# Sample attention of a hybrid decoder step taken by pairs of tokens, with the whole-array steps of a run ahead of its column products

## The chip, the cores and the metric

The kernel runs on one core of a Trainium2 chip. The metric is the device time of one execution in microseconds (us): the median of three timed runs of the kernel before is 2583.79 us (2583.14 to 2585.33). Engines are named as in the profile: PE is TensorE's matmul (PEld its weight load), DVE VectorE, ACT ScalarE, POOL GpSimd, SP SyncE.

## The reference

One step of a two-layer decoder trunk is computed for a prompt of 256 tokens and for 8 sample sequences of 4 new tokens each, which share all weights. Layer 0 mixes tokens by sparse attention: an indexer picks 256 keys for each query token out of 2048 cached ones (in pages) and the sequence's new ones, and grouped attention (16 heads on 4 key heads) runs over the picked rows alone. Layer 1 mixes by a convolution module; each layer is followed by a feed-forward block. The part that the change touches is the attention itself, of the samples and of the prompt:

```python
def attend_selected(q, k_sel, v_sel, valid):
    qg = q.reshape(tq, N_KV_HEADS, N_HEADS // N_KV_HEADS, HEAD_DIM)
    s = jnp.einsum('tngd,tsnd->tngs', qg, k_sel) * (HEAD_DIM ** -0.5)
    s = jnp.where(valid[:, None, None, :], s, -jnp.inf)
    p = jax.nn.softmax(s, axis=-1)
    o = jnp.einsum('tngs,tsnd->tngd', p, v_sel)
    return o.reshape(tq, N_HEADS * HEAD_DIM)

def one_seq(q_s, qi_s, wi_s, ki_s, k_new, v_new, pages):      # each sample sequence
    idx, valid = index_select(qi_s, wi_s, ki_s, pos_new, key_pos, k_sel)
    ...
    k_s = jnp.where(in_past, cache_k[phys, off], k_new[new_idx])
    v_s = jnp.where(in_past, cache_v[phys, off], v_new[new_idx])
    return attend_selected(q_s, k_s, v_s, valid)
```

Everything is float32. The outputs are the trunk's result, the new keys, values and indexer keys, and the new convolution states.

## The kernel before, in words

Activations are held with features on partitions and all 288 tokens (256 of the prompt, 32 of the samples) in the free dimension. Weights are streamed from HBM in slabs of 512 KB. `K.pump` loads slabs ahead (up to `k.R` of them) and splits each into a high and a low part (up to `k.S` ahead): ACT writes `wh` (L179), DVE, or POOL for a few slabs, writes `wl` (L181). A product with a weight is three PE products (L258 to L260). Each engine runs its instructions in the order in which the program emits them.

The projections of layer 0 and the selection of keys come first. Then comes the attention stage, with PSUM divided into eight banks: three named `tr`, two `sc`, two `m` and one `q`. Its work is of two kinds.

- **The samples.** For each of 32 tokens (8 sequences `b`, 4 tokens each) POOL gathers 256 selected rows of keys and values from the cache (two gathers of 128 rows, L719) into one of 11 buffers. `keys(t)` transposes the gathered keys on PE: two blocks, `c` = 0 and 1, of four 128x128 transpositions (L1340), each block in a `tr` bank, copied to `KT` by ACT for block 0 (L1345) and by DVE for block 1 (L1343). `scores(t)` multiplies with the token's queries, each key head into 16 rows of a 32-row strip of one `sc` bank (L1361); the first token of a sequence also puts a mask there (L1353, from 32 rows of `selB` and `mbS`) and the scores of the new keys (L1356). Such products use 16 or 32 columns of the array: the program places them as column tiles of 128x32, four side by side, and the mask as a row tile. After the fourth token `values(b)` takes the softmax of the sequence: maximum on DVE (L1369, L1370), exponential with its sum on ACT (L1372), reciprocal on DVE (L1374), three transpositions of the result on PE (L1378, L1379) into an `m` bank, copied by ACT (L1389) and DVE (L1387) to `PTz` and by DVE to `zn` (L1390), then the product with the new values (L1395, tiles of 32x32) and with the gathered ones, token by token (L1402, column tiles). The sum is scaled on DVE to `os` (L1407), transposed (L1411) and copied to the output `ot` (L1414).
- **The prompt.** The generator `filler` has eight units, four key heads for each of two blocks of 128 queries. `qk` adds a mask and multiplies queries with keys (L1281, L1282) into a `tr` bank, DVE takes maxima (L1284, L1285), ACT the exponentials (L1287, 128 wide in the first four units, 256 wide in two parts in the others); `norm` scales them on DVE (L1263, L1265), `turn` transposes them on PE (L1294) for a copy by ACT (L1296), and `weigh` multiplies with the values (L1304) into the `q` bank, copied by ACT (L1307). All of these PE steps use the whole array.

The two kinds are woven by hand. A loop over tokens emits for each block of `keys` one step of the pending `values` generators and `fill(FILL)`, which adds `FILL` = 0.44 us to an account and emits pieces of `filler` (each of 0.6 to 1.5 us by the author's figures) as long as the account is positive; after the token's two blocks come the scores of the token before. At token 24 three slabs of the next product's weights are split in one go. After the last token the rest of `values` and `filler` is emitted; `split_o` (L1461, L1462) then splits the output for the product with `w_attn_out`, which starts as soon as its first row block is split.

Everything after that, about 85% of the time, is products with weights; these lines are the same before and after.

Of the kernel before, what the change touches and what calls it, by code (L numbers as in the profile page):

```python
# [40 lines left out]
FILL = 0.44  # L41
# [592 lines left out]
def trunk(ctx, tc, a, o, stages=9):  # L634
# [226 lines left out]
    def prepare():  # L861
# [305 lines left out]
    vs = ap.tile([32, 512], F32, name="vs")  # L1167
# [27 lines left out]
    def turn_v(gi):  # L1195

        for tt in range(3):
# [4 lines left out]
            dst = (vt[:, tt] if tt < 2 else vs)[:, 256 * gi:256 * gi + 256]  # L1202
# [49 lines left out]
    nc.sync.dma_start(o["v"][TP:], vs)  # L1252
# [78 lines left out]
    KT, SC = {}, {}  # L1331

    def keys(t):

        kt = cp.tile([128, NKV, KSEL_S], F32, name="KT", bufs=2)
        for c in range(2):
            p = bank("tr", 3)
            g = kvt[t][:, c]
            for h in range(NKV):
                nc.tensor.transpose(p[:, h * 128:(h + 1) * 128], g[:, h * 128:(h + 1) * 128], ident)  # L1340
            dst, src = kt[:, :, c * 128:(c + 1) * 128], p[:, :512].rearrange("p (h s) -> p h s", h=NKV)
            if c:
                nc.vector.tensor_copy(dst, src)  # L1343
            else:
                nc.scalar.activation(dst, src, AF.Copy)  # L1345
            yield
        KT[t] = kt

    def scores(t):
        b, i = t // TS, t % TS  # L1350
        if i == 0:
            SC[b] = p = bank("sc", 2)
            nc.tensor.matmul(p[:, :KSEL_S + 32], selB[96:128, b], mbS[96:128], start=True, stop=False,  # L1353
                             skip_group_check=True)
# [4 lines left out]
        p, kt = SC[b], KT.pop(t)  # L1359
# [4 lines left out]
    def values(b):  # L1364
# [6 lines left out]
        yield 1  # L1371
        nc.scalar.activation(P, p[:, :KSEL_S + 32], AF.Exp, bias=mx, scale=SCALE, accum_out=sm)  # L1372
        yield 1
        nc.vector.reciprocal(sm, sm)  # L1374
        yield 1
# [5 lines left out]
        zn = cp.tile([32, 128], F32, name="zn")  # L1381
        for c in range(2):
# [3 lines left out]
            if c:  # L1386
                nc.vector.tensor_copy(dst, src)  # L1387
            else:
                nc.scalar.activation(dst, src, AF.Copy)  # L1389
        nc.vector.tensor_copy(zn, p[:32, 256:384])  # L1390
        yield
        yield
        po = bank("m", 2)
        for h in range(NKV):
# [33 lines left out]
    def step():  # L1428
        for g_ in list(vq):
            if next(g_, 0) == 0:  # L1430
                vq.remove(g_)
# [602 lines left out]
```

## Time and profile before

| what | value |
|---|---|
| median of three timed runs | 2583.79 us (2583.14 to 2585.33) |
| the profiled execution's own time | 2567.41 us |
| its span, first to last instruction | 2565.6 us |
| busy PE, DVE, ACT, POOL in the span | 99%, 63%, 46%, 25% |
| granted TensorE clock, mean | 0.994 |
| attention stage, first key transposition to the first product of `w_attn_out` | 262.13 to 373.79 us |

The profile is of one execution; its time is 1.8 us above its span, and 16 us below the median of the timed runs. In a row of the timeline stand the start, the duration from there to the end of the last of the instructions taken together, the engine, the line, the operation, out<-in, the shape and the count; in brackets the idle time of the engine before and what ended it. PE's instructions overlap: from the start of one row to the start of the next is what the first takes of the engine, and its duration is longer. An fp32 product stands as two records, a transposition as one.

### The profile page before, as it was taken

The page shows a single profiled execution, that of the slowest core. Times are in us where ns is not written, and L with a number is a line of the kernel's source. Part 1 is how long each engine was busy: PE and PEld are TensorE (multiplying, and loading weights), DVE is VectorE, ACT ScalarE, POOL GpSimd, SP SyncE. Part 2 cuts the span into 40 slices and gives each one's busy share as a digit, 9 for nine tenths or more (in the row PEclk, how much of TensorE's full clock was granted, in tenths as well). Part 3 has the DMA queues.
Part 4 walks back from the last instruction along what each step waited for, and adds up shares of the span by engine and source line. Part 5 has one row for each costly group of instructions (what it writes and reads, how often), then busy time and mean ns, then how long its engine had stood idle before and what let it go on. Part 6 is the DMA issues. An engine that isn't in the chain of part 4 may idle for free.

```text
span 2565.6 us, 48371 instructions
## 1 busy us (share of the span) xinstructions
PE 2527.9 (99%) x19614; PEld 2437.1 (95%) x19614; DVE 1612.3 (63%) x2490; ACT 1171.6 (46%) x1858; POOL 654.1 (25%) x917
## 2 busy tenths in 40 slices
PE   9999999999999999999999999999999999999997
PEld 8889669999999999999999887999999999999997
DVE  5678556776665455555669997778555444555554
ACT  4464444554443334444446444656444333444444
POOL 2153732522221100101245564352111000111123
PEclk9999999999999999999999999999999999999999
DMA  9835955564545545556455655555555455555653
GB/s 347 209 127 189 344 206 204 160 204 160 169 161 173 164 159 171 161 169 172 163 164 177 176 162 182 164 163 164 170 163 168 165 157 172 164 165 164 171 165 103
DMA packets 151503, 454.80 MB, mean 177 GB/s; under 512 B 26112, under 2 KB 46512, under 8 KB 150000
## 3 DMA queue, kind: packets, MB, share of 16 engines
q1 hardware_dynamic: 138736, 400.04, 49.3%
q0 software_dynamic: 12016, 51.09, 5.8%
q8 instruction: 153, 2.51, 0.4%
q14 instruction: 70, 0.57, 0.1%
q10 hardware_dynamic: 528, 0.59, 0.1%
HBM read 438.37 MB, written 13.30 MB: 176 GB/s over the span
## 4 chain that ended last, share of the span: by engine, by line
PE 91%; DVE 5%; ACT 2%; POOL 1%; issue 1%; DMA 0%; SPq 0%; ACTq 0%; DVEq 0%; POOLq 0%
PE pt L260 26%; PE pt L259 26%; PE pt L258 26%; PE pg L258 2%; PE pg L260 2%; PE pg L259 2%; DVE wl L181 2%; PE tr L1340 1%; PE pt L1820 1%; PE m L1402 1%; DVE cy L1804 1%; PE pg L925 1%; PE sc L1361 1%; ACT wh L179 1%; PE q L1304 0%
## 5 line engine op out<-in xcount | busy, mean ns | idle before, releaser
L181 DVE TENSOR_TENSOR wl<-raw,wh 128x1024 fp32r<-128x1024 f32 (+1 forms) x707 | 882.7, 1251 | 752.1 <-ACT wh L179 748.6
L179 ACT ACTIVATE wh<-raw 128x1024 fp32r<-128x1024 f32 (+1 forms) x726 | 760.8, 1051 | 839.4 <-PE pt L259 691.5
L260 PE MATMUL pt<-xh,wl 128*128 128x288 f32 (+1 forms) x3520 | 1040.4, 296 | 3.4 <-DVE wl L181 3.3
L258 PE MATMUL pt<-xh,wh 128*128 128x288 f32 (+1 forms) x3520 | 1042.5, 296 | 0.9 <-ACT xh L1461 0.9
L259 PE MATMUL pt<-xl,wh 128*128 128x288 f32 (+1 forms) x3520 | 1042.5, 296 | 0.1
L258 PEld LDWEIGHTS pt<-xh,wh 128*128 128x128 f32 x3520 | 663.4, 188 | 7.8 <-issue 5.8
L260 PEld LDWEIGHTS pt<-xh,wl 128*128 128x128 f32 x3520 | 666.1, 189 | 5.0 <-DVE wl L181 5.0
L259 PEld LDWEIGHTS pt<-xl,wh 128*128 128x128 f32 x3520 | 664.0, 189 | 0.5 <-DVE xl L1462 0.3
L260 PE MATMUL pt<-hh,wl 128*128 128x288 f32 (+1 forms) x1664 | 495.2, 298 | 0.0
L259 PE MATMUL pt<-hl,wh 128*128 128x288 f32 (+1 forms) x1664 | 493.7, 297 | 0.0
L258 PE MATMUL pt<-hh,wh 128*128 128x288 f32 (+1 forms) x1664 | 492.8, 296 | 0.0
L1577 POOL COPY sto<-gpad 128x2 f32<-128x2 f32 x88 | 85.1, 967 | 970.2 <-ACT gpad L1570 970.1
L259 PEld LDWEIGHTS pt<-hl,wh 128*128 128x128 f32 x1664 | 313.9, 189 | 0.2
L258 PEld LDWEIGHTS pt<-hh,wh 128*128 128x128 f32 x1664 | 313.4, 188 | 0.2
L260 PEld LDWEIGHTS pt<-hh,wl 128*128 128x128 f32 x1664 | 312.8, 188 | 0.0
L258 PE MATMUL pg<-xh,wh 128*128 128x288 f32 (+1 forms) x528 | 164.9, 312 | 2.2 <-ACT xh L283 1.2
L260 PE MATMUL pg<-xh,wl 128*128 128x288 f32 (+1 forms) x528 | 157.6, 298 | 1.4 <-DVE wl L181 1.3
L259 PE MATMUL pg<-xl,wh 128*128 128x288 f32 (+1 forms) x528 | 157.5, 298 | 0.1
L1581 ACT ACTIVATE s<-y,pvec 128x304 f32<-128x304 f32 x88 | 48.5, 551 | 161.0 <-DVE y L1576 161.0
L258 PEld LDWEIGHTS pg<-xh,wh 128*128 128x128 f32 (+1 forms) x528 | 99.8, 189 | 11.9 <-issue 7.9
L259 PEld LDWEIGHTS pg<-xl,wh 128*128 128x128 f32 (+1 forms) x528 | 99.6, 189 | 3.6 <-issue 2.6
L260 PEld LDWEIGHTS pg<-xh,wl 128*128 128x128 f32 (+1 forms) x528 | 99.8, 189 | 3.1 <-DVE wl L181 3.1
(367 smaller groups left out, 2285.7 us busy)
## 6 DMA issues: line engine op xcount, KB each, us to landing
raw<-w SPq DMA_DIRECT2D x713, 512.0 KB, 3.5
xt<-spread SPq DMA_DIRECT2D x60, 136.0 KB, 4.0
kid<-kvt POOLq DMA_DIRECT2D x4, 1024.0 KB, 6.4
kvt<-kid SPq DMA_DIRECT2D x8, 512.0 KB, 11.4
x<-xT POOLq DMA_DIRECT2D x1, 2304.0 KB, 9.9
raw<-w SPq DMA_DIRECT2D x6, 384.0 KB, 3.0
out_y<-x SPq DMA_DIRECT2D x16, 144.0 KB, 1.8
hist<-scT POOLq DMA_DIRECT2D x4, 544.0 KB, 5.6
```

What stands on the lines that cost most here:

```text
L179: nc.scalar.activation(wh[:, :n], r[:, :n], AF.Copy)
L181: eng.tensor_tensor(wl[:, :n], r[:, :n], wh[:, :n].bitcast(F32), op=OP.subtract)
L258: nc.tensor.matmul(out, wh[:, c:c + w], xh, start=st, stop=False)
L259: nc.tensor.matmul(out, wh[:, c:c + w], xl, start=False, stop=False)
L260: nc.tensor.matmul(out, wl[:, c:c + w], xh, start=False, stop=sp)
L925: nc.tensor.matmul(p[:, :512], qb[:, pr], kx[pr][:, 512 * i:512 * i + 512], start=True, stop=True)
L1340: nc.tensor.transpose(p[:, h * 128:(h + 1) * 128], g[:, h * 128:(h + 1) * 128], ident)
L1361: nc.tensor.matmul(p[32 * h:32 * h + 16, :KSEL_S], qz[b % 2][:, i, h], kt[:, h], start=False, stop=(i == TS - 1), skip_group_check=True)
L1402: nc.tensor.matmul(po[32 * h:32 * h + 16, :128], z[:, c, i, h], g[:, 512 + h * 128:640 + h * 128], start=False, stop=(i == TS - 1 and c == ...
L1577: nc.gpsimd.tensor_copy(sto[:, j, 0:2], gp[:, 256:258])
L1581: nc.scalar.activation(s[:, :304], y[:, :304], AF.Silu, bias=k.par(bc, j))
L1804: nc.vector.scalar_tensor_tensor(acc, src, w, pl if q_ == NACT else acc, op0=OP.mult, op1=OP.add)
```

## The change

The loop over tokens becomes a loop over pairs of tokens (`p_`). A pair first emits all steps that use the whole array and then all column products:

- both tokens' blocks of `keys` (four times four transpositions); in a sequence's first pair, between them, the mask (now a product of all 128 rows, with zeros written into the upper 96 rows of `selB` and `mbS` by POOL), the exponential of the sequence before, its reciprocal and the three transpositions of the softmax, and the transposition of `os` for the sequence two before;
- then `fill` with 1.7 us of `filler` (0.8 us where no keys are left);
- then the products with values for two tokens of the sequence before, and the scores of the pair's own two tokens.

The product with the new values uses 128 rows (`zn` and `vs` have zeros below row 32), so it is a column tile of 128x32 like its neighbours. Both copies to `PTz` are made by DVE. The three slabs are split one at a time, at the start of pairs 12, 13 and 14. The work is the same in kind and number: 256 key transpositions, 128 products for scores, 256 for values, and the same eight units of the prompt.

```diff
-FILL = 0.44
+FILLS = (0.8, 1.7)
...
+        nc.gpsimd.memset(selB[0:96], 0.0)
+        nc.gpsimd.memset(mbS[0:96], 0.0)
...
-    vs = ap.tile([32, 512], F32, name="vs")
+    vs = ap.tile([128, 512], F32, name="vs")
+    nc.gpsimd.memset(vs, 0.0)
...
+    def masked(b):
+        SC[b] = p = bank("sc", 2)
+        nc.tensor.matmul(p[:, :KSEL_S + 32], selB[:, b], mbS, start=True, stop=False, skip_group_check=True)
...
-            nc.tensor.matmul(p[:, :KSEL_S + 32], selB[96:128, b], mbS[96:128], start=True, stop=False,
-                             skip_group_check=True)
...
-            if c:
-                nc.vector.tensor_copy(dst, src)
-            else:
-                nc.scalar.activation(dst, src, AF.Copy)
-        nc.vector.tensor_copy(zn, p[:32, 256:384])
...
+            nc.vector.tensor_copy(dst, src)
+        nc.vector.tensor_copy(zns[b % 2][:32], p[:32, 256:384])
...
-    for t in range(n_t + 1):
-        if t == n_t - 8:
-            k.pump(g_out[0].first)
...
-            for _ in keys(t):
-                step()
-                if t:
-                    fill(FILL)
...
-        if t:
-            scores(t - 1)
-            if t % TS == 0:
-                vq.append(values(t // TS - 1))
-                next(vq[-1])
...
+    for p_ in range(2 * NB + 3):
+        b, odd = p_ // 2, p_ % 2
+        if 0 <= p_ - 2 * NB + 4 < k.S:
+            k.R, k.S, rs_ = k.R - k.S + p_ - 2 * NB + 5, p_ - 2 * NB + 5, (k.R, k.S)
             k.pump(g_out[0].first)
+            k.R, k.S = rs_
+        if not odd:
+            if 0 <= b - 1 < NB:
+                soft[b - 1] = softmax(b - 1)
...
+        if live:
+            keys(t, 0)
+        if turning:
+            exped(*soft[b - 1])
+        if live:
+            keys(t, 1)
+            if not odd:
+                masked(b)
+        if turning:
+            sm = soft[b - 1][1]
+            nc.vector.reciprocal(sm, sm)
+        if live:
+            keys(t + 1, 0)
+        else:
+            fill(FILLS[0])
+        if turning:
+            turned_ps(b - 1, soft[b - 1][0])
+        if live:
+            keys(t + 1, 1)
+        if not odd and 0 <= b - 2 < NB:
+            out_rows(b - 2, os_)
+        if p_:
+            fill(FILLS[1] if live else FILLS[0])
+        if 0 <= b - 1 < NB:
+            values(b - 1, 2 * odd)
+            values(b - 1, 2 * odd + 1)
+        if live:
+            scores(t)
+            scores(t + 1)
```

The first place is PE's order in the middle of the stage. Before, around the values of the second sequence (the number behind a name is that of the buffer; `tr`, `sc`, `m` and `q` are the PSUM banks, `kvt` and `kvx` the gathered rows, `PTz` and `zn` the transposed softmax, `KT` the copied keys, `P` and `PT` the prompt's), it stands so:

```order
L1340 MATMUL tr_3553<-ident_109,kvt_3370 128x128 x4
L1395 MATMUL m_3559<-vs_268,zn_3521 32x128 x4
L1402 MATMUL m_3559<-kvt_3079,PTz1_3076 16x128 x8
L1304 MATMUL q_3577<-PT_3450,vt_267 128x512
L1294 MATMUL tr_3580<-ident_109,P_3380 128x128 x4
L1340 MATMUL tr_3587<-ident_109,kvt_3370 128x128 x4
L1402 MATMUL m_3559<-kvt_3084,PTz1_3076 16x128 x8
L1361 MATMUL sc_3497<-KT_3507,qz0_3073 16x256 x4
L1340 MATMUL tr_3612<-ident_109,kvt_3412 128x128 x4
L1402 MATMUL m_3559<-kvt_3089,PTz1_3076 16x128 x8
```

After, in pair 6 (counted from 0 as `p_` is), which turns the third sequence's softmax, it stands so:

```order
L1383 MATMUL m_3666<-ident_109,Ps_3634 128x128 x2
L1384 MATMUL m_3666<-ident_109,Ps_3634 32x128
L1344 MATMUL tr_3673<-ident_109,kvt_3408 128x128 x4
L1411 MATMUL m_3679<-ident_109,os_3639 128x128
L1307 MATMUL q_3682<-PT_3513,vt_267 128x512
L1297 MATMUL tr_3685<-ident_109,P_3487 128x128 x4
L1398 MATMUL m_3692<-vs_268,zn0_3126 32x128 x4
L1405 MATMUL m_3692<-kvx_3080,PTz0_3078 16x128 x8
L1405 MATMUL m_3692<-kvx_3081,PTz0_3078 16x128 x8
L1360 MATMUL sc_3656<-kT_266,qn_270 16x32 x4
L1365 MATMUL sc_3656<-KT_3642,qz1_3077 16x256 x4
```

Before, column products (L1395, L1402, L1361) stand between blocks of four transpositions; after, the products with the new values, with two tokens' values and the scores of two tokens stand in one run behind all that uses the whole array. In the whole stage column products form 47 runs before and 18 after.

The second place is DVE's order at the start of the stage, where the first units of the prompt (`mx`, `sm` and `P`) meet the first softmax (`mxs`). Before:

```order
L1284 TENSOR_REDUCE mx_3193<-tr_3194 128x4
L1285 TENSOR_SCALAR mx_3193<-mx_3193 128x4
L1343 COPY KT_3179<-tr_3209 128x4x128
L1446 MEMSET PTz1_3076 128x512
L1343 COPY KT_3220<-tr_3227 128x4x128
L1440 COPY qz1_3074<-qn_269 128x4x4x4
L1263 RECIPROCAL sm_3192<-sm_3192 128x4
L1265 TENSOR_SCALAR P_3191<-P_3191,sm_3192 128x128 x4
L1284 TENSOR_REDUCE mx_3259<-tr_3260 128x4
L1285 TENSOR_SCALAR mx_3259<-mx_3259 128x4
L1343 COPY KT_3245<-tr_3275 128x4x128
L1369 TENSOR_REDUCE mxs_3286<-sc_3169 128x1
```

After:

```order
L1287 TENSOR_REDUCE mx_3201<-tr_3202 128x4
L1288 TENSOR_SCALAR mx_3201<-mx_3201 128x4
L1266 RECIPROCAL sm_3200<-sm_3200 128x4
L1268 TENSOR_SCALAR P_3199<-P_3199,sm_3200 128x128 x4
L1287 TENSOR_REDUCE mx_3224<-tr_3225 128x4
L1288 TENSOR_SCALAR mx_3224<-mx_3224 128x4
L1373 TENSOR_REDUCE mxs_3249<-sc_3145 128x1
L1374 TENSOR_SCALAR mxs_3249<-mxs_3249 128x1
L1443 COPY qz1_3077<-qn_270 128x4x4x4
L1347 COPY KT_3254<-tr_3262 128x4x128
```

Before, a copy of keys (`KT`) stood behind each unit's maxima. After, two units' maxima, and the scaling of `P` between them, stand ahead of the first sequence's maximum (L1373) and of the next copy of keys.

More of the change, by code (lines that the diff above doesn't have):

```diff
@@ L1362, in scores, with softmax @@
                              stop=(i == TS - 1), skip_group_check=True)
-    def values(b):
+    def softmax(b):
         p = SC.pop(b)
@@ L1385, in values, with out_rows @@
             dst = diag(z, 256 * c)
[L1386 to L1394, printed above, removed]
-            nc.tensor.matmul(po[32 * h:32 * h + 32, :128], zn[:, 32 * h:32 * h + 32], vs[:, h * 128:(h + 1) * 128],
-                             start=True, stop=False, skip_group_check=True)
-        for i in range(TS):
-            kv = kvt.pop(TS * b + i)
-            for c in range(2):
-                g = kv[:, c]
-                for h in range(NKV):
-                    nc.tensor.matmul(po[32 * h:32 * h + 16, :128], z[:, c, i, h], g[:, 512 + h * 128:640 + h * 128],
-                                     start=False, stop=(i == TS - 1 and c == 1), skip_group_check=True)
-            kv_load(1)
-            yield
-        os_ = cp.tile([128, 128], F32, name="os")
-        nc.vector.tensor_scalar(os_, po[:, :128], sm, None, op0=OP.mult)
-        yield
-        yield
+            nc.vector.tensor_copy(dst, src)
+        nc.vector.tensor_copy(zns[b % 2][:32], p[:32, 256:384])
+    def values(b, i):
+        z, zn = PTz[b % 2], zns[b % 2]
+        if i == 0:
+            PO[b] = bank("m", 2)
+            for h in range(NKV):
+                nc.tensor.matmul(PO[b][32 * h:32 * h + 32, :128], zn[:, 32 * h:32 * h + 32],
+                                 vs[:, h * 128:(h + 1) * 128], start=True, stop=False, skip_group_check=True)
+        po = PO[b]
+        kv = kvt.pop(TS * b + i)
+        for c in range(2):
+            g = kv[:, c]
+            for h in range(NKV):
+                nc.tensor.matmul(po[32 * h:32 * h + 16, :128], z[:, c, i, h], g[:, 512 + h * 128:640 + h * 128],
+                                 start=False, stop=(i == TS - 1 and c == 1), skip_group_check=True)
+        kv_load(1)
+    def out_rows(b, os_):
         p = bank("m", 2)
@@ L1452, in trunk @@
-    while vq:
-        step()
-        fill(FILL)
+    NB = NS
+    soft, os_ = {}, {}
+    nc.vector.memset(zns[0], 0.0)
+    nc.vector.memset(zns[1], 0.0)
+    for p_ in range(2 * NB + 3):
+        b, odd = p_ // 2, p_ % 2
+        if 0 <= p_ - 2 * NB + 4 < k.S:
+            k.R, k.S, rs_ = k.R - k.S + p_ - 2 * NB + 5, p_ - 2 * NB + 5, (k.R, k.S)
+            k.pump(g_out[0].first)
+            k.R, k.S = rs_
+        if not odd:
+            if 0 <= b - 1 < NB:
+                soft[b - 1] = softmax(b - 1)
+            if 0 <= b - 2 < NB:
+                sm = soft.pop(b - 2)[1]
+                os_ = cp.tile([128, 128], F32, name="os")
+                nc.vector.tensor_scalar(os_, PO.pop(b - 2)[:, :128], sm, None, op0=OP.mult)
+            if b < NB:
+                nc.vector.tensor_copy(diag(qz[b % 2], 0), qn[:, :, TS * b:TS * b + TS].rearrange("p h t g -> p t h g"))
+        if p_ in (0, 1):
+            nc.vector.memset(PTz[p_], 0.0)
+        t = 2 * p_
+        live = b < NB
+        turning = not odd and 0 <= b - 1 < NB
+        if live:
[11 more added lines that the diff above has]
+            keys(t + 1, 0)
+        else:
+            fill(FILLS[0])
[13 more added lines that the diff above has]
+            scores(t + 1)
```

51 lines of the change are left out of this document (19 added, 32 removed).

## The prediction

> **What bounds the kernel now.** I read the page first, then the busy time by windows, then PE's timeline through the stage that changes, then the rows of ACT and DVE there.
>
> ```profile
> span 2565.6 us, 48371 instructions
> PE 2527.9 (99%) x19614; PEld 2437.1 (95%) x19614; DVE 1612.3 (63%) x2490; ACT 1171.6 (46%) x1858; POOL 654.1 (25%) x917
> 262.10:373.80 111.70, 108.54 (x1363) 70.96 (x1361) 61.25 (x170) 51.61 (x146) 64.71 (x101) 1.00 0.80 291
> ```
>
> PE bounds the whole, and the attention stage too: 108.5 of its 111.7 us (third row: PE, PEld, DVE, ACT and POOL in that order). What comes after the stage is unchanged work that waits for PE, so what the stage gains or loses the kernel gains or loses. DVE with 61 us and ACT with 52 are not bounds in sum.
>
> How PE's time in the stage is made shows in its starts. These are rows of two places:
>
> ```profile
> 286.85 0.60 PE L1294 MATMUL tr<-ident,P 128*128 128x128 f32 x4
> 287.29 0.60 PE L1340 MATMUL tr<-ident,kvx 128*128 128x128 f32 x4
> 287.82 0.63 PE L1402 MATMUL m<-kvt,PTz 128*16 128x128 f32 x16
> 288.27 0.61 PE L1361 MATMUL sc<-KT,qz 128*16 128x256 f32 x8
> 288.81 1.09 PE L1340 MATMUL tr<-ident,kvx 128*128 128x128 f32 x8
> ...
> 311.23 0.60 PE L1294 MATMUL tr<-ident,P 128*128 128x128 f32 x4
> 311.76 0.63 PE L1361 MATMUL sc<-KT,qz 128*16 128x256 f32 x8
> 312.31 0.66 PE L1340 MATMUL tr<-ident,kvt 128*128 128x128 f32 x4
> 312.90 0.63 PE L1402 MATMUL m<-kvx,PTz 128*16 128x128 f32 x16
> 313.46 0.66 PE L1340 MATMUL tr<-ident,kvt 128*128 128x128 f32 x4
> ```
>
> Four transpositions before more whole-array work take 0.44 us (286.85 to 287.29). Before column products they take 0.53 (to 287.82), and between two runs of column products 0.59 (312.31 to 312.90). Sixteen value records take 0.45 before more column products, 0.56 before whole-array work. So one visit to column products costs 0.09 going out, 0.11 coming back and 0.06 at the second transposition: 0.26 us, whatever it holds.
>
> **The change part by part.** *Fewer visits.* The order has 47 runs of column products before and 18 after with the same products in them: 29 visits less, 29 x 0.26 = 7.5 us.
>
> *New values and mask.* Both use 32 rows, and so change the array once more inside a visit:
>
> ```profile
> 307.56 0.42 PE L1395 MATMUL m<-vs,zn 32*32 32x128 f32 x8
> 307.91 0.63 PE L1402 MATMUL m<-kvx,PTz 128*16 128x128 f32 x16
> 309.12 0.66 PE L1340 MATMUL tr<-ident,kvt 128*128 128x128 f32 x4 [0.58 <-DVE KT L1343]
> ```
>
> Eight records of new values take 0.35 us here. Half of sixteen in the stream would take 0.22. As column tiles they save 0.13, times 8 sequences 1.0 us. The mask, moved among transpositions as a product of all rows, saves one change, 0.11 by the rows above, less what it may cost more there, which no row shows: 0 to 0.11 each. I take 0.08, as its 288 columns stay the same; together 0.7. Gross gain: 7.5 + 1.0 + 0.7 = 9.2 us.
>
> By the rows the price is one of changing the array's division, not of the products. [...]
>
> *Old waits that go.* PE's waits in the stage before:
>
> ```profile
> 270.26 0.66 PE L1340 MATMUL tr<-ident,kvt 128*128 128x128 f32 x4 [0.53 <-DVE KT L1343]
> 271.27 0.66 PE L1294 MATMUL tr<-ident,P 128*128 128x128 f32 x4 [0.35 <-ACT P L1287]
> 342.06 1.14 PE L1340 MATMUL tr<-ident,kvt 128*128 128x128 f32 x8 [0.48 <-ACT KT L1345]
> 343.91 0.63 PE L1361 MATMUL sc<-KT,qz 128*16 128x256 f32 x8 [0.30 <-DVE KT L1343]
> ```
>
> With the 0.58 at 309.12 that is 2.2 us of idle inside the stage. Start to start it is more: 307.91 to 309.12 is 1.21 for a run worth 0.56, so 0.65 for the 0.58. I take 3.0 in all. None of these places stands in the new order, so all 3.0 go.
>
> *New waits.* Where the pieces were mixed, a softmax had several blocks of other work between its steps. Now its chain lies inside one run of transpositions:
>
> ```profile
> 300.92 0.66 PE L1340 MATMUL tr<-ident,kvt 128*128 128x128 f32 x4
> 301.06 0.46 DVE L1369 TENSOR_REDUCE mxs<-sc 128x1 f32<-128x288 f32 x1 [0.33 <-PE sc L1361]
> 301.66 0.60 ACT L1345 ACTIVATE KT<-tr 128x512 f32<-128x512 f32 x1 [2.13 <-PE tr L1340]
> 302.16 0.50 ACT L1372 ACTIVATE Ps<-sc,mxs 128x288 f32<-128x288 f32 x1
> 302.54 0.20 ACT L1372 ACTIVATION_READ_ACCUMULATOR Ps<-sc,mxs 128x1 f32 x1
> ```
>
> From the first transposition behind the scores to the end of the exponential are 1.82 us (300.92 to 302.74). In a pair that turns a softmax, PE now has three blocks and the mask between: 0.50 + 0.44 + 0.20 + 0.44 = about 1.55. It then waits 0.3, with the handing over 0.4, and longer by all that ACT or DVE is late. In pairs 4, 6 and 10 they are free in time: 3 x 0.4 = 1.2 us.
>
> They are late where the prompt's units stand just ahead:
>
> ```profile
> 263.47 0.22 PE L1281 MATMUL tr<-pm,identN 128*128 128x128 bf16 x1
> ...
> 264.80 0.60 PE L1340 MATMUL tr<-ident,kvt 128*128 128x128 f32 x4
> 265.00 0.69 DVE L1284 TENSOR_REDUCE mx<-tr 128x4 f32<-128x512 f32 x1 [0.95 <-PE tr L1282]
> 265.99 0.37 ACT L1287 ACTIVATE P<-tr,mx 128x128 f32<-128x128 f32 x1 [1.75 <-DVE mx L1285]
> 267.37 0.61 ACT L1345 ACTIVATE KT<-tr 128x512 f32<-128x512 f32 x1
> 267.74 1.09 DVE L1265 TENSOR_SCALAR P<-P,sm 128x128 f32<-128x128 f32 x4
> ```
>
> ```profile
> L1265 DVE TENSOR_SCALAR P<-P,sm 128x256 f32<-128x256 f32 x16 | 6.0, 433 | 0.1
> L1287 ACT ACTIVATE P<-tr,mx 128x256 f32<-128x256 f32 x16 | 7.5, 470 | 17.3 <-PE m L1402 8.3 <-DVE mx L1285 6.0 <-DVE KT L1343 3.0
> L181 DVE TENSOR_TENSOR wl<-raw,wh 128x1024 fp32r<-128x1024 f32 x3 | 3.5, 1220 | 2.1 <-ACT wh L179 2.1
> L1390 DVE COPY zn<-m 32x128 f32<-32x128 f32 x8 | 2.1, 269 | 0.0
> L1387 DVE COPY PTz<-m 128x64 f32<-128x64 f32 x8 | 1.8, 224 | 5.2 <-ACT PTz L1389 5.2
> ```
>
> (The last five are means by shape, in ns behind the comma.) A unit of 128 keys takes PE 1.33 us (263.47 to 264.80). If its products end at time e, it has its maxima from e + 0.2, its exponentials from e + 1.2 to e + 2.6, and its scaling from e + 2.9 to e + 4.0.
>
> - *Pair 2* (pairs counted from 0). Pair 1 ends with two units. The second one's maxima stand on DVE behind the first one's scaling: from e + 4.0. Behind them come the first softmax's maximum (0.46), the queries' copy and the copy of pair 2's second block (all in the second order of DVE above, 0.7 for a copy by the 0.69 of a reduction of the same size), which so ends at about e + 6.1. PE reaches pair 2 at e + 1.33 for the second unit + 1.1 for two tokens' scores (0.54 for one at 288.27, 0.11 of it coming back, and 0.15 for going) = e + 2.4, and its third block 1.1 later. All three `tr` banks are then unread (the unit's until e + 6.3, the block's until e + 6.1): a wait of 2.6. The exponential comes behind the second unit's exponentials and a copy on ACT, at e + 7.4: another 0.8. Together 3.4.
> - *Pair 8.* Pair 7 ends with two parts of 256 keys, and a unit's scaling between their maxima. From the first part's e the exponentials (2 x 0.47 and the reads) end at e + 2.2, the scaling (4 x 0.43, less some overlap) at e + 3.9, the next maxima at e + 4.6 and the next exponentials at e + 5.9. They hold the bank that pair 8's third block takes. PE is there after the second part (1.1), two tokens' values and scores (2.0) and two blocks with the mask (1.1), at e + 4.2: a wait of 1.7, and 0.5 for the softmax. Together 2.2.
> - *Pairs 12 and 14.* The slab's split stands on DVE ahead of the maximum: 1.22 for `wl`, begun with the pair. Some 0.46 of it is hidden behind ACT's first copy, the rest is late: 0.85 each, 1.7.
> - *The end* (pairs 16 to 18), where no keys are left to cover: after the last turn of a softmax its copies (0.22 + 0.22 + 0.27, less the one transposition between), 0.6; after the last turn of the prompt the copy of 0.60 by ACT with its start and end, 0.8. Together 1.4.
> - *Start and bank handovers.* DVE's zeroing of four tiles ahead of the first copies, 0.4; a dozen block starts 0.05 behind the bank's reader, and one unit's scaling in pair 14: 0.9. Together 1.3.
>
> Sum: 1.2 + 3.4 + 2.2 + 1.7 + 1.4 + 1.3 = 11.2 us. The rows bound it: nothing, if every step were done in time, and 21.5 if every turn behind pair 2 waited as in pair 8 (3.4 + 7 x 2.2 + 1.4 + 1.3). I take the walk's value, as its rows are those of the instructions concerned.
>
> *What costs nothing, or little.* The stage's end before:
>
> ```profile
> 372.61 0.27 PE L1411 MATMUL m<-ident,os 128*128 128x128 f32 x1
> 373.79 0.40 PE L258 MATMUL pt<-xh,wh 128*128 128x288 f32 x1 [0.91 <-ACT xh L1461]
> ```
>
> Behind the prompt's last product (ahead of 372.61) a copy and a split on ACT lead to the first product with weights. They do so in the new order too, without the transposition of 0.11 that now comes earlier: 0.1. POOL's three memsets stand long before the gathers, while POOL idles. Freed buffers come at most a pair later than before, with 11 of them; a late gather would cost what it is late.
>
> Net: -9.2 - 3.0 + 11.2 + 0.1 = -0.9. Walked in this way the waits of before come out short, too (the 0.58, where multiplications were slow, is not in the means); I add 0.4 for such. The forecast is -0.5 us: 2566.9 for the profiled execution's 2567.4 (2565.6 of span and 1.8 around), and 2583.8 - 0.5 = **2583.3 us** for the median of the runs, which lies 16 us above for things outside the span.
>
> **The rivals.** A change of 0.2%, about 5.2 us, is what a measurement of this kernel can tell.
>
> *Faster: the waits stay as they were.* If the copies and exponentials are done in time, as in most places before (3.0 in 111.7 us), the gross gain stands: 2583.8 - 9.2 = 2574.6. Against it: the exponential's 1.82 us are in the rows, and only 1.55 of work covers them. Up to 6.5 us of waits in place of the old 3.0 (9.2 + 3.0 - 0.1 - 0.4 - 5.2) the kernel is faster by 5.2 or more.
>
> *Slower: ACT's queue is late at each turn of a softmax.* Place: the third block and the turn in pairs 2, 4, ... 16. Price: as in pair 8, 2.2 instead of 0.4 to 0.85, so the upper bound of 21.5: -9.2 - 3.0 + 21.5 + 0.1 + 0.4 = +9.8, 2593.6. It decides from 17 us of waits on. For it: six even pairs have some unit's exponentials close ahead. Against: in most of them scores and values of 2 us lie between. [...]
>
> *The visits' price isn't saved*, if it hangs on the products' weights and not on the change. Then the 7.5 is missing, net +7.0: 2590.8. Against: the stream of 0.45 and 0.44 has a new weight for each product.
>
> **How the numbers follow.** Chances: forecast, within 0.2%, 0.73; faster 0.18, as somewhat under half of the waits gone is enough for it; late at each turn 0.06 and visits not saved 0.03, so slower 0.09. Low end 2577.5: waits of about 5.5. High end 2588.5: waits of 16.4, a turn or two less late than in the slower rival. That leaves the far parts of the rivals out, under 2 in 10.
>
> **What would show it.** In the new profile: 18 visits to column products; PE's longest wait in pair 2 (over 2 us), on a copy of `KT`, the next in pair 8 on the prompt's exponentials; a wait of 0.3 to 0.9 for `Ps` at nearly each turn. The stage should take about 111 us. It is wrong if PE's idle time in the stage is under 6 or over 15 us, or if a visit still costs 0.26 per token.

## The result and the profile after

The changed kernel took 2619.13 us (median of 4 runs, 2617.29 to 2619.86) beside 2583.47 us of before (4 runs, 2580.77 to 2585.33): 1.0126 times as long, 95% interval 1.0114 to 1.0138. That is 35.7 us slower. The forecast was 2583.3 with a range up to 2588.5.

The page of the profile after puts the loss in one place. Span, TensorE's row, and two rows of the 40 slices (65 us each):

```profile
span 2617.8 us, 48379 instructions
PE 2543.4 (97%) x19614; PEld 2454.9 (94%) x19614; DVE 1612.5 (62%) x2500; ACT 1170.9 (45%) x1850; POOL 657.2 (25%) x920
PE   9999679999999999999999999999999999999997
PEclk9999889999999999999999999999999999999999
```

Only the fifth and sixth slice fall, and in them the clock falls too. They hold most of the attention stage. In one window from its first key transposition to the first product with `w_attn_out` (columns as in the prediction: PE, PEld, DVE, ACT, POOL, granted clock, DMA share, GB/s):

```profile
264.20:423.80 159.60, 121.47 (x1363) 85.50 (x1360) 60.62 (x180) 51.37 (x138) 63.97 (x101) 0.87 0.59 204
```

159.6 us where the first profile of before has 111.7, with the same busy time on DVE and ACT. PE is idle for 38 us. The granted clock is either 1.00 or 0.50 in these records, so at a mean of 0.87 it ran 0.13 x 159.6 x 2 = 41 us at half speed. The four largest of PE's waits in the stage (total, times, longest):

```profile
PE tr L1344 <- ACT KT L1349: 12.4, 5, 3.6
PE tr L1344 <- issue: 6.8, 3, 3.3
PE m L1383 <- ACT Ps L1378: 5.1, 4, 2.2
PE sc L1365 <- DVE KT L1347: 3.8, 2, 2.4
```

The first two lines are not in the forecast. One such place, pair 3, on PE, then ACT, then POOL:

```profile
292.78 1.05 PE L1365 MATMUL sc<-KT,qz 128*16 128x256 f32 x16
293.76 1.09 PE L1344 MATMUL tr<-ident,kvt 128*128 128x128 f32 x8
294.69 0.60 PE L1344 MATMUL tr<-ident,kvx 128*128 128x128 f32 x4
298.60 0.69 PE L1344 MATMUL tr<-ident,kvx 128*128 128x128 f32 x2 [3.31 <-issue]
```

```profile
294.02 0.21 ACT L1290 ACTIVATION_READ_ACCUMULATOR P<-tr,mx 128x1 f32 x1
297.95 0.60 ACT L1349 ACTIVATE KT<-tr 128x512 f32<-128x512 f32 x1 [3.72 <-remote]
```

```profile
297.08 0.95 POOL L719 DMA_INDIRECT kvt<-kvc,idxS  x1 [0.16 <-issue]
```

The first key block's four transpositions are done by 294.4 (half of the eight that begin at 293.76). ACT has been idle since 294.2, and copies them only at 297.95. PE, with three blocks in the three `tr` banks, stands until that copy is done. So the copy isn't slow and ACT isn't late: PE's result reaches ACT 3.5 us after PE's rows say that it is made. POOL's row is the last of four gathers in a row (from 292.77); the copy starts as it ends. The same program in a later series of runs:

```profile
283.63 1.09 PE L1344 MATMUL tr<-ident,kvt 128*128 128x128 f32 x8
284.56 1.13 PE L1344 MATMUL tr<-ident,kvx 128*128 128x128 f32 x8
```

```profile
284.39 0.60 ACT L1349 ACTIVATE KT<-tr 128x512 f32<-128x512 f32 x1 [0.28 <-PE tr L1344]
```

Here the copy starts 0.1 us behind the fourth transposition. I call a result "late" when the first reading of it starts over half a microsecond behind its row's end though the reader is free. By this measure 25 of the 64 copies of key blocks in the profile after are late, by up to 3.8 us, and each of the 25 starts while POOL issues a run of gathers or within 1.2 us behind one. In after_again none is (0.4 us at most).

One thing is needed to read the rest. The eight series of runs fall into two groups by the time of the kernel *before*: 2567 to 2568 us in five of them, 2583 to 2587 in three (the first comparison and the last two series). So each time stands beside the before of its own series; I call the two "quiet" and "late" surroundings. It is not one chip against another: on each of two chips one series was quiet and another, later one late. In time the five quiet series lie between the first comparison and the last two. The first profile of before (2567.4 us) is of the quiet kind, the runs beside it (2583.8) of the other. Where that comes from, and what it does to this change, is what most experiments turned to. Most medians are of 8 to 10 runs; those of after_fill_pair0 and both_again are of 4, of after_more_traffic and fewer_gathers_again of 3, of before_more_traffic and after_no_pause of 2. One of the ten runs of before_128_rows took 8682.64 us; it is in the median but not in the ratio.

| kernel | its median, us | before beside it | ratio, 95% interval |
|---|---|---|---|
| before_again | 2568.68 | 2568.11 | 1.0005 (0.9995 to 1.0015) |
| after_fewer_gathers | 2570.69 | 2568.11 | 1.0009 (0.9999 to 1.0019) |
| before_fewer_gathers | 2567.35 | 2568.11 | 0.9998 (0.9988 to 1.0007) |
| before_128_rows | 2566.97 | 2568.11 | 0.9993 (0.9983 to 1.0003) |
| after_again | 2570.82 | 2566.88 | 1.0014 (1.0004 to 1.0024) |
| after_fill_pair0 | 2578.35 | 2567.86 | 1.0042 (1.0026 to 1.0059) |
| after_fill_mid | 2573.44 | 2567.86 | 1.0023 (1.0014 to 1.0033) |
| after_more_traffic | 2580.42 | 2567.86 | 1.0045 (1.0029 to 1.0061) |
| before_more_traffic | 2581.52 | 2567.86 | 1.0052 (1.0032 to 1.0072) |
| after_turn_late | 2567.03 | 2567.86 | 0.9994 (0.9985 to 1.0004) |
| after_fill_parity | 2567.33 | 2567.86 | 0.9996 (0.9986 to 1.0005) |
| after_both | 2563.08 | 2567.86 | 0.9980 (0.9971 to 0.9990) |
| after_third | 2572.93 | 2567.80 | 1.0019 (1.0008 to 1.0030) |
| before_third | 2567.18 | 2567.80 | 1.0003 (0.9991 to 1.0014) |
| after_no_pause | 2623.80 | 2586.86 | 1.0144 (1.0115 to 1.0174) |
| before_no_pause | 2587.06 | 2586.86 | 1.0001 (0.9990 to 1.0012) |
| both_again | 2599.09 | 2585.85 | 1.0049 (1.0032 to 1.0066) |
| fewer_gathers_again | 2575.25 | 2585.85 | 0.9955 (0.9940 to 0.9971) |

### The profile page after: what moved, and what is told of

Same layout as the page of the kernel before. It is cut to its first block, busy times and chain, and to the rows that moved or that the text cites. A ratio compares the mean times of both kernels' runs of the same rounds, so it can differ in the third digit from the quotient of the medians.

```text
span 2617.8 us, 48379 instructions
## 1 busy us (share of the span) xinstructions
PE 2543.4 (97%) x19614; PEld 2454.9 (94%) x19614; DVE 1612.5 (62%) x2500; ACT 1170.9 (45%) x1850; POOL 657.2 (25%) x920
## 4 chain that ended last, share of the span: by engine, by line
PE 88%; DVE 5%; ACT 2%; issue 1%; another core or an unknown queue 1%; POOL 1%; DMA 1%; SPq 0%; ACTq 0%; DVEq 0%; POOLq 0%
PE pt L260 25%; PE pt L259 25%; PE pt L258 25%; PE pg L258 2%; PE pg L260 2%; PE pg L259 2%; DVE wl L181 2%; PE pt L1843 1%; PE tr L1344 1%; DVE cy L1827 1%; ACT wh L179 1%; PE pg L927 1%; PE m L1405 1%; PE tr L1285 0%
## 5 line engine op out<-in xcount | busy, mean ns | idle before, releaser
L179 ACT ACTIVATE wh<-raw 128x1024 fp32r<-128x1024 f32 (+1 forms) x726 | 760.9, 1051 | 842.3 <-PE pt L259 694.9
```

What stands on the lines that cost most here:

```text
L179: nc.scalar.activation(wh[:, :n], r[:, :n], AF.Copy)
```

## The experiments

### Is it the gathers?

The kernel before again, both kernels with fewer gathers, and the 128-row products alone. In the first, nothing is edited. "Fewer gathers" edits the loading of a token (the same lines in both kernels):

```diff
             i = t % RING
+            if t >= RING:
+                kvt[t] = first[i]
+                kvt["pos"] += 1
+                continue
...
             kvt[t] = g
+            first.append(g)
```

**before_again.** 

> The kernel before, unchanged, for a second profile: the first one took 2567.4 us, while its runs took 2580.8 to 2585.3. Theory 'gathers' (while POOL issues gathers, PE's results reach ACT and DVE late, PE idles and its clock falls): the runs near 2583 have such a stage, so this profile takes about 2583, its attention stage is 16 us longer than the 111.7 of the first, and PE waits for copies of KT there. Rival 'waits' (the kernel after has the softmax and copy waits of the forecast, only larger): the first profile is typical, the stage is 112 us again.

Measured: 2568.68, no late copies of keys, a stage of 111.1 us. The theory's 2583 did not come, and the rival's 112 us did. But this decides nothing between the two: the runs of before beside it took 2568.11, so the surroundings had changed for before as well.

**after_fewer_gathers.** 

> The kernel after, with gathers for the first 11 tokens alone; the later tokens use these buffers again, so two thirds of the cached keys and values are those of other tokens. Theory 'gathers': the late results go from pair 3 on, the stage falls from 159.5 to some 120 us (the first two pairs still run beside gathers), the time to about 2580. Rival 'waits': the waits stay, the time stays within 3 us of 2619. Third, 'late buffers' (gathers come too late because their buffers come free late): the same fall as in 'gathers', but then no result was late in the kernel after, only data.

Measured: 2570.69, in quiet surroundings. That is a fall further than the 2580 of "gathers", and "late buffers" expected it too; what it meant had to wait for after_again.

**before_fewer_gathers.** 

> The kernel before, with gathers for the first 11 tokens alone (the later tokens use these buffers again, so two thirds of the keys and values are those of other tokens). Theory 'gathers': what separates its runs (2583) from its first profile (2567) goes: about 2567 to 2570. Rival 'waits': no change, 2583 within 2.

Measured: 2567.35, as "gathers" expected, but no different from its before. Where results are not late, the 42 gathers left out are worth nothing to before (ratio 0.9998, 0.9988 to 1.0007): their transfers are hidden.

**before_128_rows.** 

> The kernel before, with only the new values and the mask as products of 128 rows (zeros added, three memsets on POOL, two on DVE). By the forecast's terms 1.7 us less than before, 2581 to 2583. Rival: the 128-row products themselves cost, or their memsets move something before the stage: over 2588.

The edit, in short:

```diff
-    vs = ap.tile([32, 512], F32, name="vs")
+    vs = ap.tile([128, 512], F32, name="vs")
+    nc.gpsimd.memset(vs, 0.0)
...
-            nc.tensor.matmul(p[:, :KSEL_S + 32], selB[96:128, b], mbS[96:128], start=True, stop=False,
+            nc.tensor.matmul(p[:, :KSEL_S + 32], selB[:, b], mbS, start=True, stop=False,
...
-        zn = cp.tile([32, 128], F32, name="zn")
+        zn = zns[b % 2]
```

Measured: 1.1 us under its before by the medians, with an interval that holds both zero and the 1.7, so the times don't decide. Its stage in the profile took 110.1 us with 3.4 of waits, that of before_again 111.1 with 2.5: without waits 1.9 us less in this one pair of profiles, near the forecast's 1.7.

### Is it the kernel or its surroundings?

**after_again.** 

> The kernel after, unchanged, beside runs of before that are here near 2568 as in its first profile. Theory 'gathers' (PE's results come late while gathers run, because of how the kernel after bunches its work): the time is again 45 to 52 us above before, 2613 to 2620, with waits of 3 to 4 us in nearly each pair. Rival 'surroundings' (what makes PE's results late was in the surroundings of the first comparison, where before too took 16 us more than its profile): the run with few gathers already has the whole of it, 2570 to 2573, with 2.7 us of waiting in pair 2 and 0.2 to 0.3 at each turn of a softmax, and no late results.

Measured: 2570.82 beside 2566.88, ten runs from 2568.1 to 2575.4. The rival holds. In quiet surroundings the change costs 3.9 us (interval 1.0 to 6.2), not 35.7. Its stage takes 114.4 us, and its waits are those of the forecast:

```profile
262.87:377.28 114.41, 104.29 (x1363) 76.61 (x1361) 62.11 (x180) 50.89 (x138) 64.09 (x101) 0.97 0.78 284
```

```profile
PE tr L1344 <- DVE KT L1347: 2.7, 1, 2.7
PE m L1383 <- ACT Ps L1378: 2.2, 6, 0.7
PE tr L1344 <- ACT P L1290: 2.1, 1, 2.1
PE pt L258 <- ACT xh L1484: 1.0, 1, 1.0
PE q L1307 <- ACT PT L1299: 0.6, 1, 0.6
PE m L1398 <- DVE zn L1391: 0.6, 1, 0.6
PE sc L1365 <- DVE KT L1347: 0.5, 1, 0.5
PE tr L1344 <- ACT KT L1349: 0.2, 1, 0.2
```

**after_third** and **before_third**, unchanged once more. 

> The kernel after, unchanged, a third time. If what held PE's results up in the first comparison goes with the surroundings, the time follows that of before: near 2571 where before takes 2567, near 2619 where it takes 2583. If it is a state that the kernel after falls into by itself, some of its runs take over 2600 where before takes 2567.

> The kernel before, unchanged, for its profile beside the run above. Where it takes 2583 its own results should come late while gathers run, for some 16 us in all; where it takes 2567 none should.

Measured: 2572.93 and 2567.18 beside 2567.80, quiet again. None of the unedited changed kernel's 18 runs in quiet surroundings came near 2600 (2575.43 at most), and none of the 15 quiet profiles, of whatever kernel, has a late copy of keys: the changed order doesn't fall into that state by itself.

### What is worth what, in quiet surroundings

**after_fill_pair0.** 

> The kernel after, with a piece of the prompt in pair 0 too, so that pair 1 no longer ends with two units. Theory 'waits plus clock': the wait of 2.7 us in pair 2 falls under 1, and so does the half clock of 3.4 us behind it (about 1.7 us of work lost): 3 to 4 us less than after, so 2566 to 2568 where before takes 2567. Rival 'clock apart' (the clock falls for another reason): half clock stays at that place and 2 us are won at most.

```diff
-        if p_:
-            fill(FILLS[1] if live else FILLS[0])
+        fill(FILLS[1] if live else FILLS[0])
```

Measured: 2578.35, 7.5 us more than after_again (6.6 if each is taken beside its own before) instead of 3 to 4 less. Both theories fail on the sum. The waits of pair 2 did shrink (0.48 and 0.32 us), but one unit earlier shifts every later one, and the same collision stands elsewhere. The stage's waits come to 14.6 us instead of 9.9. The five that matter here:

```profile
271.41 1.62 PE L1344 MATMUL tr<-ident,kvt 128*128 128x128 f32 x8 [2.38 <-DVE KT L1347]
278.56 0.66 PE L1344 MATMUL tr<-ident,kvt 128*128 128x128 f32 x4 [0.48 <-ACT P L1290]
311.95 1.09 PE L1344 MATMUL tr<-ident,kvt 128*128 128x128 f32 x8 [1.76 <-ACT P L1290]
343.69 0.69 PE L1383 MATMUL m<-ident,Ps 128*128 128x128 f32 x2 [2.25 <-ACT Ps L1378]
360.13 0.44 PE L1383 MATMUL m<-ident,Ps 128*128 128x128 f32 x2 [2.51 <-ACT Ps L1378]
```

**after_fill_mid.** 

> The kernel after, with the prompt's piece of each pair ahead of the turn of the softmax (behind the third key block) instead of ahead of the column products, from pair 0 on. Theory 'waits plus clock': every wait of the stage but those at its start and end goes, with both stretches of half clock, so idle in the stage falls from 9.9 us to 3 or 4 and the time to 2560 to 2563, 4 to 7 us under before. Rival 'price' (a visit to column products does not cost 0.26 us): the waits go, but the time stays within 2 us of before.

```diff
         if live:
             keys(t + 1, 0)
-        else:
-            fill(FILLS[0])
+        fill(FILLS[1] if live else FILLS[0])
...
-        if p_:
-            fill(FILLS[1] if live else FILLS[0])
+        if not live:
+            fill(FILLS[0])
```

Measured: 2573.44, some 10 us above the 2560 to 2563 of the theory. The waits for `Ps` shrank from 2.2 to 1.0 us, but the prompt's maxima and scaling now stand on DVE ahead of the softmax's own copies, and those are waited for instead: 14.0 us in the stage where 3 or 4 were expected. The two largest of PE's waits:

```profile
PE m L1398 <- DVE zn L1391: 5.8, 6, 3.1
PE sc L1365 <- DVE KT L1347: 3.4, 2, 2.9
```

Here I walked the queues of PE, ACT and DVE once more over the rows' durations, as in the forecast, for other places of the turn and other shares of the prompt per pair. Two edits stood out.

**after_turn_late.** 

> The kernel after, with the turn of a softmax behind the fourth key block of its pair instead of ahead of it. Theory 'covers' (each wait is the chain's length less the work that lies over it, as in the forecast): the waits for Ps of 0.2 to 0.3 go, those of pairs 2 and 8 stay; 2.5 us less than after, 2568 to 2569 where before takes 2567. Rival 'same total' (the wait only moves to the copies behind the turn): within 1 us of after, 2570 to 2572.

```diff
-        if turning:
-            turned_ps(b - 1, soft[b - 1][0])
         if live:
             keys(t + 1, 1)
+        if turning:
+            turned_ps(b - 1, soft[b - 1][0])
```

Measured: 2567.03, 3.8 us less than after_again (4.8 if each is taken beside its own before), where 2.5 were expected. "Covers" holds: the waits for `Ps` fell from 2.2 to 0.4 us. The rest was not foreseen: pair 8 waits 1.7 us instead of 2.1, and the clock doesn't fall behind it.

**after_fill_parity.** 

> The kernel after, with 2.3 us of the prompt asked for in even pairs and 0.4 in odd ones (1.7 in each now), and 1.2 at the end, so that the prompt's units stand behind a turn and not ahead of the next. Theory 'covers': pair 2 waits 0.5 to 1.3 instead of 2.9, pair 8 under 1, no half clock: 5 us less than after, 2565 to 2567. Rival 'same total': the waits move to other pairs, 2570 to 2574, as they did when pair 0 took a piece.

```diff
-FILLS = (0.8, 1.7)
+FILLS = (1.2, 2.3, 0.4)
...
-            fill(FILLS[1] if live else FILLS[0])
+            fill(FILLS[1 + odd] if live else FILLS[0])
```

Measured: 2567.33, 3.5 us less than after_again (4.5 if each is taken beside its own before). That is just above the 2565 to 2567 of "covers" and well below the 2570 to 2574 of "same total"; the granted clock is 1.00 through the stage.

**after_both.** 

> Both edits together. Theory 'covers': 7 to 8 us less than after, 2562 to 2565, 2 to 5 us under before. Rival 'same total': 2568 to 2572.

Measured: 2563.08 beside 2567.86, 0.9980 (0.9971 to 0.9990): faster than both kernels, and where the walk had put it (2562 to 2565). Its stage takes 106.1 us at full clock:

```profile
261.60:367.70 106.10, 100.90 (x1362) 74.68 (x1360) 60.77 (x180) 50.23 (x138) 64.50 (x101) 1.00 0.79 307
```

### What makes results late?

**after_more_traffic** and **before_more_traffic.** 

> The kernel after, with 6 MB of DMA from DRAM to DRAM added on SP's queue at the start of the stage (nothing reads what it writes). Theory 'traffic' (in the first comparison other traffic held PE's results up while gathers ran): PE's results come late again, up to 3 us, while the gathers run, and the time is 10 to 50 us above 2571. Rival: the gathers land later, PE waits only where their data are late, and no result comes late: under 2590.

> The kernel before with the same 6 MB. Theory 'traffic': late results here too, but half the cost of the kernel after or less. Rival: as there, only late data: the same extra time as the kernel after within 5 us.

```diff
+    junk = tc.dram_tile([12 * 128, 1024], F32, name="junk")
+    for i in range(12):
+        nc.sync.dma_start(junk[128 * i:128 * i + 128], a["w"][131072 * i:131072 * i + 131072].rearrange("(p c) -> p c", c=1024))
```

Measured: 2580.42 and 2581.52, the rival in both. No copy of keys comes late; PE waits where its data do. In the kernel after, then in before:

```profile
PE tr L1347 <- DMA kvt<-kvc,idxS: 6.5, 2, 6.3
```

```profile
PE tr L1343 <- DMA kvt<-kvc,idxS: 9.3, 3, 3.4
```

This is what a shortage of data looks like: the wait names the gather. In the first comparison it names a copy, or nothing, but for one wait of 2.1 us. Names are weaker evidence there, as records are missing from those profiles (last section); that data were there is shown where PE had already transposed them and the copy was late, as in pair 3.

**after_no_pause** and **before_no_pause.** 

> The kernel after without the memset that follows each gather on POOL, so that gathers are issued every 1.1 us instead of 1.43. Theory 'gather issue' (PE's results come late when gathers are issued faster than they can be worked off; in the first comparison something had slowed that working off): late results of over 0.5 us appear here while gathers run, with time above 2580. Rival: none come late; the first data land no sooner, since the DMA engines are busy at 1.43 us already, and the time stays at 2570 to 2573.

> The kernel before without that memset. Theory 'gather issue': late results here too, 2575 to 2590. Rival: 2567 within 2.

```diff
                 gather(g[:, c], a["kvc"], idxS[:, 32 * c + t:32 * c + t + 1])
-
-                nc.gpsimd.memset(pause, 0)
```

This series met late surroundings, as its before shows (2586.86). So it says nothing about the pause but that it is worth nothing there to before (1.0001), and after_no_pause (two runs, 1.0144) comes near the first comparison (1.0126). Theory "gather issue" is left undecided. But before_no_pause gives a profile of the order of before in late surroundings, with the time of before:

```profile
263.80:393.00 129.20, 114.96 (x1362) 72.90 (x1360) 58.63 (x169) 51.81 (x146) 47.97 (x51) 0.97 0.69 246
```

Its stage takes 129.2 us instead of 111.1: that is where the runs at 2584 to 2587 lose the 16 to 19 us, inside the span (2585.2 us of this execution's 2587.0). Late results stand in it too: 13 of the 64 copies of keys, by up to 3.8 us. DVE's maximum of the first unit, whose products PE has done by 266.6:

```profile
266.19 0.44 PE L1281 MATMUL tr<-kT,x 128*128 128x128 f32 x2
```

```profile
270.08 0.69 DVE L1283 TENSOR_REDUCE mx<-tr 128x4 f32<-128x512 f32 x1 [4.37 <-remote]
```

**both_again** and **fewer_gathers_again**, the last two, met late surroundings as well. 

> The kernel after with the turn behind the fourth key block and the prompt's pieces by even and odd pairs, again. Beside a before of 2567: 2563, as measured. Beside a before of 2584 to 2587 (late results while gathers run, as in the first comparison): theory 'no cover' (a late result costs what the order has no other work for) gives more than before again, 2600 to 2620, as its blocks of keys stand in a row like those of the kernel after; rival 'own waits' (the kernel after lost there through the same two waits as elsewhere): below before, 2580 to 2584.

Measured: 2599.09 beside 2585.85, just under the 2600 to 2620 of "no cover" and far above the rival's 2580 to 2584. The order that is 4.8 us faster than before in quiet surroundings is 13.2 us slower than it here, though it is still 22 us nearer to before than the change as it was made. In its profile 30 of the 64 copies of keys are late:

```profile
264.00:404.50 140.50, 109.92 (x1363) 78.83 (x1361) 60.02 (x180) 50.27 (x138) 64.20 (x101) 0.95 0.66 231
```

> The kernel after with gathers for the first 11 tokens alone, again (two thirds of its keys and values are those of other tokens). Beside a before of 2567: 2571. Beside a before of 2584 to 2587: if gathers are what makes results late there, late results only up to the end of the gathers at about 275 us, and 2575 to 2582; if something else is, late results from pair 3 on as well, and over 2600.

Measured: 2575.25, 10.6 us less than the kernel before beside it, which does all its gathers; before with few gathers was not run in late surroundings. POOL's last gather begins at 272.93 us; the stage up to 274.9 and behind it:

```profile
262.90:274.90 12.00, 7.26 (x74) 5.55 (x73) 4.67 (x13) 2.57 (x5) 10.18 (x17) 1.00 0.98 378
274.90:379.80 104.90, 95.86 (x1290) 69.91 (x1290) 55.09 (x168) 48.23 (x133) 0.00 (x0) 0.98 0.16 57
```

While gathers are issued (POOL 10.2 us) PE is busy 7.3 of 12.0 us; behind them it is busy 95.9 of 104.9, with waits much like those of after_again. All six late copies of keys belong to blocks done by 272.4; none follows. So late results need gathers under way. In quiet surroundings (after_fewer_gathers) the same twelve microseconds show none.

## Why the prediction was wrong

**The step that failed** is one sentence: that the median of the runs "lies 16 us above for things outside the span". The profiled execution was of the quiet kind, the runs were not, and the 16 us were inside the stage that the change reorders. before_no_pause shows it: 129.2 us of stage, 1.8 us around the span. The kernel before itself, unedited, says the same in the last two series: its 17 runs of 2583.6 to 2590.8 us have spans only 1.7 to 2.0 us shorter. Every term of the sum came from rows of the quiet kind and was added to a median of the other. In quiet surroundings the same change gave +3.9 and +5.1 us where -0.5 was forecast; the other 30 us and more came with the late results.

**What that hid.** The walk took a result as ready 0.2 us behind its product. In the first comparison 25 of 64 key blocks are read late, by 0.6 to 3.8 us, while gathers are issued or within 1.2 us behind, and they are issued for 70 of the stage's 159.6 us, in runs up to 395 us. An order should then be as good as the work it has between a product and the next step that waits for its reading. The order of before had one or two key blocks and then a unit or a turn, from other chains. The new one puts three or four key blocks in a row at the head of each pair, into three banks: behind the third PE has nothing to do that doesn't hang on a late result. Late results cost 18 us in before's order, 45 in the new one (159.6 less 114.4 of after_again) and 34 in after_both (140.5 less 106.1). Of the 45, 28 are waits (37.8 in all, 9.9 in after_again) and 17 are longer busy time for the same instructions, at the lower clock. That cover is the cause of the difference is argued, not shown: the orders also differ in how many key blocks are read late (13, 25 and 30), and no run separates the two.

**Gathers as "nothing, or little".** I put their cost at lateness of data. Where it can be seen, as in pair 3, the data were in time; it was PE's results that came late under them. The row that could have warned was not in the profile of before, which has no late result. The 16 us could have.

**The gross gain, 9.2 us.** after_turn_late is the order without the recurring wait for `Ps`. Its stage is 109.9 us with 7.7 of waits and one stretch of 3.4 us at half clock; before_again has 111.1 with 2.5. Without waits that is 6.5 us less, about 8 with the clock. If the 128-row part gave its 1.7, 29 visits gave some 5 to 6 us, 0.16 to 0.22 us each instead of 0.26: nearer to the price of the two changes alone (0.09 and 0.11). This rests on one profile of each order, but the rival "visits' price isn't saved" falls by it.

**The new waits, 11.2 us.** Place by place against after_again: pair 2, forecast 2.6 and 0.8, idle 2.7 and 0.2; pairs 4, 6 and 10, waits of 0.3 each, idle 0.22 to 0.23; pair 8, 1.7 and 0.5, idle 2.1 and nothing; pairs 12 and 14, 0.85 each, idle 0.68 and 0.63; the end, 0.6 and 0.8, idle 0.61 and 0.64. PE's idle time is 9.9 us, between the 6 and 15 named as limits; the stage took 114.4 us instead of about 111. For this order in quiet surroundings the mechanism was right. The method is not safe on that account: after_both came where it was placed (2562 to 2565), but the forecasts for after_fill_pair0 and after_fill_mid missed by some 10 us, as moving one unit set off collisions elsewhere.

**What the sum lacked** in quiet surroundings is the clock behind the two longest waits. Three windows of after_again, ahead of the wait of pair 2, behind it, and later:

```profile
265.60:272.10 6.50, 6.43 (x68) 4.98 (x72) 3.39 (x6) 1.88 (x6) 5.72 (x9) 1.00 1.01 379
276.52:279.93 3.41, 3.18 (x14) 2.71 (x15) 1.07 (x5) 1.71 (x6) 0.00 (x0) 0.50 1.01 400
279.93:283.00 3.07, 3.07 (x71) 2.79 (x73) 2.14 (x8) 1.00 (x4) 0.35 (x1) 1.00 1.01 398
```

For 3.41 us behind the wait the granted clock is 0.50, which costs half of the 3.2 us of work in it. The same follows the wait of pair 8: 3 us together, and -0.5 becomes +2.5, where the two series of the kernel after gave +3.9 and +5.1. (In the profile of after_third the first stretch is twice as long, 6.83 us from 274.48, worth some 1.7 us more by the same working.) Waits of 2.7 and 2.1 us, each shorter than the 3.41 us at half clock behind the first, were enough for the two falls (last section).

**The other rivals.** "Slower: ACT's queue is late at each turn" named the right sign for the wrong reason: ACT was idle when its input was late. "Faster" needed under 6.5 us of waits; the change as it was made has 9.9. after_both, another order, has 5.0, and is 4.8 us faster in quiet surroundings.

## What to carry to other kernels

When a profiled execution is faster than all timed runs, find the difference before using its rows: it may lie in the stage that the change touches. Count, for each product, the independent work behind it before PE needs its reading; an order with little of it is fast only where results come at once (here a stage of 114.4 us, and 159.6 where they came late). Grouping work of one kind saves changes of the array's division, but it sorts the steps of one chain next to each other, and what it saves per visit here (some 0.2 us) is used up by the shortest uncovered wait (0.22 us).

## What the runs showed that was not expected

- PE's results can reach ACT and DVE late, with both idle and the data there, while POOL issues gathers: by up to 3.8 us in the profile after, 5.3 us in after_no_pause. In the same program at other times they are read within 0.4 us. It goes with the surroundings (three series of eight, two of them on chips that were quiet earlier), needs gathers under way, and was not brought about by 6 MB of added DRAM traffic in quiet surroundings. What does it is open; a run without gathers' own landing signals was not tried.
- In those profiles many landing events are missing as well. The list of DMA issues has a landing time for the gathers of `kvt` in after_again, and none in the profile after, as it gives none for a semaphore with a record missing:

```profile
kvt<-kvc,idxS POOLq DMA_INDIRECT x42, 5.9
```

```profile
kvt<-kvc,idxS POOLq DMA_INDIRECT x42
```

  The records themselves say where. The eight semaphores on which POOL's transfers land have 1051 updates between 230 and 420 us in after_again and 734 between 230 and 450 us in the profile after, whose stage ends later; outside these stretches 383 and 384. So of these, events were lost just where gathers run and results are late. Lost events alone don't show whether the recording held PE up, and no run here tells, as none is known to have run without the recording.
- A wait of 2 to 3 us can cost another 1.5 us by the clock, or nothing, and the records show which. In all 20 profiles the granted clock changes only on a grid of 3.41 us, fixed for the execution. These are the steps around the two longest waits of after_again, then around the first (2.85 us) and the longest (3.07 us) wait of after_fill_mid; the first number behind the length is PE's busy time:

```profile
273.11:276.52 3.41, 0.72 (x7) 0.43 (x7) 3.17 (x11) 1.28 (x7) 1.27 (x3) 1.00 1.00 376
314.07:317.48 3.41, 1.33 (x12) 1.04 (x11) 3.34 (x11) 1.41 (x6) 2.92 (x5) 1.00 1.03 360
```

```profile
266.44:269.85 3.41, 1.88 (x28) 1.20 (x25) 1.70 (x8) 1.51 (x8) 3.08 (x6) 1.00 0.96 372
269.85:273.27 3.42, 2.10 (x21) 1.56 (x22) 2.13 (x5) 2.11 (x9) 2.92 (x6) 1.00 1.01 401
307.40:310.81 3.41, 1.33 (x52) 1.32 (x56) 2.63 (x10) 1.03 (x4) 0.39 (x1) 1.00 0.87 333
```

  Half clock follows the steps with 0.72, 1.33 and 1.33 us of busy time, and not those with 1.88 and 2.10: the wait of 2.85 us is cut in two by the grid, the others lie wholly or for the most part in one step. Over the 946 steps at full clock between 241 and 416 us in the 20 profiles, all 41 in which PE is idle for 1.86 us or more are followed by half clock, and 2 of the other 905. So in these runs what a wait costs by the clock hangs on how much of it falls into one step; where the grid lies is luck. The wait of 1.7 us in pair 8 of after_turn_late leaves 1.66 us of busy time in its step, and no fall follows.
